# Weight-block sums for a Winograd-form down projection: added up in DRAM by accumulating transfers, instead of on VectorE

## The chip, the cores and the metric

The kernel runs on one core of a Trainium2 chip. A core has a matrix engine (TensorE, PE in the profile, with its weight loads as PEld), a vector engine (VectorE, DVE), an activation engine (ScalarE, ACT), a general engine (GpSimd, POOL) and a queue engine (SyncE, SP). They run side by side, each through its own list of instructions in order, and wait for one another by semaphores. Sixteen DMA engines move data between DRAM and the core's memory (SBUF); SP, ACT and POOL each issue transfers on a queue of their own (q1, q10 and q0 in the profile). Time is device time in microseconds (us); a difference under about 0.2% is not told from none.

## What is computed

Two layers of a hybrid decoder over 512 positions of width 1024, in float32. Each layer adds two branches to the residual x. The first mixes positions in three ways (RWKV-7, retention, spatial gating) and merges them. The second is a gated MLP, and its last matmul in the last layer, with the final norm, is the last stage here:

```python
for l in range(DEPTH):
    h = rmsnorm(x, norm1_g[l])
    p = h @ w_in[l]
    ...
    x = x + jnp.sum(gates * proj, axis=2) @ w_out[l]
    x = x + conv_ffn(rmsnorm(x, norm2_g[l]), ffn_w_up[l], ffn_conv_w[l], ffn_conv_b[l], ffn_w_down[l])
return rmsnorm(x, final_g)
```

The down projection takes 2816 inner channels (22 blocks of 128) to 1024 outputs.

## The kernel before

Every float32 product is made of three passes in a rounded format: an operand is split into a high part (`hi`, made by ACT) and a low part (`lo`, made by DVE), and `mm3` multiplies hi by hi, hi by lo and lo by hi. Weights come as units of 128 rows by 512 columns. For each unit SP loads a raw tile `wr` of 256 KB (`load`), ACT and DVE split it (`part`), and PE uses it (`unit`). A first pass over the program writes down all units in order as a plan, and the second pass loads and splits ahead of use: `AHEAD` says how many split units may stand ahead, `NRAW` and `DEEP` how many raw ones, by the pool that the stage uses; the last stage has the pool "q", with raw tiles taken in turn from the pool of three `wr` buffers and from the general pool `u`.

The last down projection is done in a two by two block form with seven products in place of eight (Winograd's form of Strassen's method). The inner channels are taken as 11 pairs of blocks; for each pair q the weights are four blocks w0 to w3 of 128 by 512 in DRAM (`wdt`): w0 and w1 are the two column halves of the first inner block, w2 and w3 those of the second. Three of the seven products take w0, w2 and w3 as they are; four take sums of blocks, `tsum`, numbered 7, 5, 6 and 4. Each sum is a tile of 256 KB in DRAM, `ts`, 44 in all. Before the change they are made by `presum`: POOL loads the four blocks into SBUF tiles `pre` (line 253), DVE makes four sums in place (lines 242 to 245), and POOL stores them (line 248). `PRE` says at which step this happens: four pairs beside the first layer's up projection (`ffn_up`, line 1071), seven beside its down projection (`ffn_down`, line 1130). The activations' side of the form is made in `halves` in the last layer's up projection, and the products are put together in `last`.

The order of instructions on each engine is not that of the program's text. A planner goes through the program with its own estimate of durations and gives each engine the instruction whose inputs and buffers are there; the text's order only ranks what is ready. Instructions under `keep_in_program_order` and those that PE issues while `pin` is set stay in the order of the text. Each engine then runs its list in that order.

What POOL does early in layer 0 matters for the change. The first norm's reciprocal root is a power on POOL (`norm_stats`, line 267), and PE then spreads it over the rows (`norm_rows`, line 272) at a fixed place among the first projections. POOL then makes the low parts of small weights (`wus`, line 487) and of the decay and rate inputs (line 511), on which PE's groups of line 533 wait. For each of four groups of heads it masks products with affine selects (lines 579 and 580). After the fourth, `solve` copies diagonal blocks (line 771), DVE runs a recursion of 31 steps, ACT and POOL copy back (lines 769 and 771), and PE goes on with line 808.

Of the kernel before, what the change touches and what calls it, by code (L numbers as in the profile page):

```python
# [8 lines left out]
F32 = mybir.dt.float32  # L9
# [10 lines left out]
NFF = 22  # L20
# [2 lines left out]
NU, NR, NFP = 31, 16, 39  # L23
FILL = (36, 2, 1)
KEPT = 6
PRE = {(0, "f", 2): 0, (0, "f", 4): 1, (0, "f", 6): 2, (0, "f", 8): 3, (0, "d", 0): 4, (0, "d", 1): 5, (0, "d", 2): 6, (0, "d", 3): 7,
       (0, "d", 4): 8, (0, "d", 5): 9, (0, "d", 6): 10}
SEQ = "0 H 0 S 0 U S U S 0 S 0 0 S 2 2 Y 0 0 2 1 2 1 2 1 2 1 2 1 2 1 1 1"
NRAW = 3
AHEAD = {None: 2, "p": 4, "r": 3, "f": 3, "u": 5, "q": 4}  # L30
DEEP = 6
EXP_HALF = math.exp(-0.5)


# [17 lines left out]
class Emit:  # L52
# [181 lines left out]
        q.dma_start(d, t)  # L234
        return d

    def presum(self, l, stage, m):

        if self.pre:
            q, b = self.pre.pop()  # L240
            V = self.nc.vector
            V.tensor_tensor(b[3], b[3], b[1], op=SUB)
            V.tensor_tensor(b[1], b[1], b[0], op=SUB)
            V.tensor_tensor(b[0], b[0], b[3], op=ADD)
            V.tensor_tensor(b[2], b[2], b[0], op=SUB)
            for p, t in zip((7, 5, 6, 4), (b[3], b[1], b[0], b[2])):
                self.tsum[q, p] = self.dp.tile([128, 512], F32, name=self.nm("ts"))
                self.nc.gpsimd.dma_start(self.tsum[q, p], t)
        q = PRE.get((l, stage, m))
        if q is not None:  # L250
            b = self.fpre.pop(0) if stage == "f" else [self.u(n="pre") for _ in range(4)]
            for i, t in enumerate(b):
                self.nc.gpsimd.dma_start(t, self.a["wdt"][0, 2 * q + i // 2][:, i % 2 * 512:i % 2 * 512 + 512])
            self.pre.append((q, b))

    def norm_new(self):
        return {"z": [], "acc": None}
# [66 lines left out]
    def run(self):  # L324
        nc, tc, a, V = self.nc, self.tc, self.a, self.nc.vector
        self.con = self.cp.tile([128, NCC], F32, name="con")
        self.pre, self.tsum = [], {}
        self.rst = self.cp.tile([128, 512], F32, name="rst")
        self.bonesR = self.cp.tile([128, 128], F32R, name="bonesR")
        self.ones = self.cp.tile([128, 128], F32R, name="ones")  # L330
        V.memset(self.rst, 1.0)
        wu = self.acc()
        for i in range(5):
            nc.tensor.matmul(wu[:, 0:256], self.rst[:, 0:128], self.rst[:, 256:512], start=True, stop=True)
        self.pc = self.sp.tile([128, 64], F32, name="g1", tag="g1", bufs=1)
        st = self.norm_new()
        xs = [self.u(n="x") for _ in range(8)]
        self.keep = True
        with tc.high_priority():
            tc.keep_in_program_order(nc.scalar.dma_start(self.pc[:, 0:8], a["pcols"][0][:, PC["n1"]:PC["n1"] + 8]))  # L340
            for j in range(8):
                tc.keep_in_program_order((nc.scalar if j in (1, 3) else nc.sync).dma_start(xs[j], a["xT"][:, j, :]))
                if self.plan and j in (0, 2, 3):
                    self.load(self.plan[self.nraw])
        tc.keep_in_program_order(nc.scalar.copy(self.small((128, 1), "ms"), self.rst[:, 0:1]))
        tc.keep_in_program_order(nc.scalar.copy(self.ones, self.rst[:, 0:128]))
        for step in "z0 w z1 z2 z3 w w z4 z5 w z6 z7 w s0 s1 s2 w s3 s4 s5 s6 s7".split():
            if step == "w":
                if self.plan:
                    if self.nraw == self.npart:  # L350
                        self.load(self.plan[self.nraw])
                    self.part(self.plan[self.npart])
            elif step[0] == "z":
                self.norm_z(st, xs[int(step[1])], "n1")
            else:
                self.norm_sq(st, xs[int(step[1])])
        self.keep = False
        self.load_pc(0)
        tc.keep_in_program_order(nc.scalar.dma_start(self.con, a["con"]))
        xd = [a["xT"][:, j, :] for j in range(8)]  # L360
        for l in range(L):
            mg = self.mixer(l, st)
            st = self.norm_new()
            x = self.wout(l, mg, xd, st)
            st["sq"] = self.split(st["acc"])
            act = self.ffn_up(l, st, x if l == L - 1 else None)
            if l == L - 1:
                self.last(act)
            else:
                st = self.norm_new()  # L370
                x, xd = self.ffn_down(l, act, x, st)
                st["sq"] = self.split(st["acc"])
            self.rp.__exit__(None, None, None)
            self.fp = None
# [683 lines left out]
    def ffn_up(self, l, st, x):  # L1058
        nc, V, A = self.nc, self.nc.vector, self.nc.scalar
        nt = [0]  # L1060
        self.xt = []

        def at(**kw):
            nt[0] += 1
            return (self.f if nt[0] <= NFP else self.r)(dt=F32R, n="ah")

        act = []
        first = self.firstF(l, (78, 79, 80), st, (3,))
        if l == 0:
            self.fpre = [[self.f(n="pre") for _ in range(4)] for _ in range(4)]  # L1070
        for i in range(NFF):
            if l == 0 and i % 2 == 0 and 2 <= i <= 10:
                self.presum(l, "f", i)
            if x and i % 2 == 1 and i < 17:
                o = self.r(n="xt")
                self.turned(o, self.r(n="xT"), x[i // 2], nc.gpsimd)
                self.xt.append(o.rearrange("p (a c d) -> p c a d", c=4, d=32))
            cs = []
            for j in (i, NFF + i):
                ps = first.pop(0) if first else self.colF(l, 78 + 2 * i + (j >= NFF))  # L1080
                u = self.u(n="fu")
                V.tensor_tensor(u, ps, self.rsF, op=MUL)  # L1082
                t = self.u(n="cv")
                A.activation(t, u, AF.Identity, scale=self.p("cw2", j), bias=self.p("cb", j))  # L1084
                V.scalar_tensor_tensor(t[:, 1:], u[:, :511], self.p("cw1", j), t[:, 1:], op0=MUL, op1=ADD)
                V.scalar_tensor_tensor(t[:, 2:], u[:, :510], self.p("cw0", j), t[:, 2:], op0=MUL, op1=ADD)
                cs.append(t)
            g, v = cs
            th = self.u(n="fth")
            A.activation(th, g, AF.Tanh, scale=0.5)  # L1090
            V.scalar_tensor_tensor(th, th, 1.0, g, op0=ADD, op1=MUL)
            V.tensor_tensor(th, th, v, op=MUL)
            if l < L - 1:
                act.append(self.split(th, at))
            elif i % 2 == 0:
                even = th
            else:
                act.append(self.halves(even, th, i // 2, at))
        return act

    def halves(self, a, b, q, at):
# [5 lines left out]
            self.s4 = self.dp.tile([128, 512], F32, name=self.nm("s4"))  # L1107
        P.dma_start(ab[:, h[0]], a[:, h[0]])
        P.dma_start(ab[:, h[1]], b[:, h[0]])
        V.tensor_tensor(s[:, h[0]], a[:, h[1]], b[:, h[1]], op=ADD)  # L1110
        V.tensor_tensor(s[:, h[1]], s[:, h[0]], a[:, h[0]], op=SUB)
        V.tensor_tensor(d[:, h[0]], b[:, h[0]], s[:, h[1]], op=SUB)
        P.dma_start(self.s4[:, h[q % 2]], d[:, h[0]])
        V.tensor_tensor(b[:, h[0]], a[:, h[0]], a[:, h[1]], op=SUB)
        return self.split(s, at), self.split(b, at), ab, self.s4

    def ffn_down(self, l, act, x, st):
# [3 lines left out]
        for m in range(8):  # L1121
            ps = self.acc()
# [4 lines left out]
            d = self.dp.tile([128, 512], F32, name=self.nm("xd"))  # L1127
            nc.gpsimd.dma_start(d, x[m])
            xd.append(d)
            self.presum(l, "d", m)  # L1130
        return x, xd


    def last(self, act):
# [27 lines left out]
            po(A.activation(t, ps, AF.Copy, scale=0.5))  # L1162
            return t

        def addx(ps, h, c):

            y = self.f(n="v")
            for j in range(4):
                v = lambda t: t[:, 128 * j:128 * j + 128].rearrange("p (a d) -> p a d", d=32)
                x = self.xt[4 * h + j][:, c]  # L1170
                V.scalar_tensor_tensor(v(y), v(ps), 0.5, x, op0=MUL, op1=ADD)  # L1171
            return y

        def plus(y, ps, z):
            return V.scalar_tensor_tensor(y, ps, 0.5, z, op0=MUL, op1=ADD)

        def square(y, s):
            return A.activation(self.u(n="sq")[:, 0:y.shape[1]], y, AF.Square, accum_out=s)  # L1178
# [32 lines left out]
        for q in range(Q):  # L1211
# [5 lines left out]
            if q % 2 or q == Q - 1:  # L1217
                s4.append(spill(act[q][3], 512 if q % 2 else 256))
            if q < 2:
                v[2, q], v[3, q] = addx(pss[5][q], 1, 2 + q), addx(pss[5][q], 1, q)  # L1220
            elif q < 4:
                v[1, q - 2] = addx(pss[4][q - 2], 0, q)
            elif q < 6:
# [5 lines left out]
        for q in range(Q):  # L1229
# [3 lines left out]
            if q < 2:  # L1233
                plus(f0[q], out[1][q], f0[q])
                plus(v[0, q], out[1][q], v[0, q])
                plus(v[3, q], out[1][q], v[3, q])
            elif q in (2, 5):
                r = q // 5
                c, ya, yb = 2 + r, v[1, r], v[2, r]
                V.tensor_tensor(ya, ya, f0[r], op=ADD)  # L1240
                V.tensor_tensor(yb, yb, f0[r], op=ADD)
                s1, b = self.small((128, 1), "fs1"), bias[:, c:c + 1]
                square(ya, ss[:, c:c + 1])
                square(yb, s1)
# [20 lines left out]
        for r in range(2):  # L1265
            for q, w in enumerate(ws, Q - KEPT):
                go(3, q, r, w)
            y, ya, b = v[3, r], v[0, r], bias[:, r:r + 1]
            po(plus(y, out[3][r], y))
            if r == 0:  # L1270
                s = self.small((128, 1), "fs1")
                po(square(y, s))
# [131 lines left out]
```

## Time and profile before

| | us |
|---|---|
| median of 3 runs (lowest, highest) | 1713.97 (1713.09, 1715.02) |
| profiled execution | 1706.19 |
| its span, first to last instruction | 1704.5 |
| PE busy | 1687.8 |
| DVE busy | 1233.0 |
| ACT busy | 798.0 |
| POOL busy | 249.8 |

The profile is one execution. A row of a group of instructions gives line, engine, operation, tiles written and read, count, busy time and mean, and then the idle time of the engine just before them with what ended it. A row of the timeline gives start and length in us first. Rows of the DMA queues give packets, MB and the share of 16 engines' time in the stretch asked for; rows of DMA issues give size and the median time from issue to landing. PE's matmuls overlap in their pipeline, so that one of 390 ns begins about 228 ns after the one before it.

### The profile page before, as it was taken

What the parts mean: (1) busy time and instruction counts of PE and PEld (TensorE: products, weight loads), DVE (VectorE), ACT (ScalarE), POOL (GpSimd) and SP (SyncE); (2) the same over time, 40 slices, a digit from 0 to 9 for tenths busy, and PEclk for the clock granted to TensorE, in tenths of its full rate; (3) what the DMA queues carried; (4) which work ended last, traced back from release to release, by engine and by line L of the source; (5) the groups of instructions that cost most, each with busy time, mean ns of one, the idle gap of its engine ahead of it and who ended that gap; (6) DMA issues with size and microseconds to landing.
All of it is one profiled execution on the core that took longest, in us unless ns stands there. A gap on an engine that the chain in (4) does not pass through costs nothing. (4 is left out here: it accounts for less than half of the span.)

```text
span 1704.5 us, 27880 instructions
## 1 busy us (share of the span) xinstructions
PE 1687.8 (99%) x10214; PEld 1379.2 (81%) x10214; DVE 1233.0 (72%) x2157; ACT 798.0 (47%) x1367; POOL 249.8 (15%) x353
## 2 busy tenths in 40 slices
PE   9999999999999999999999999999999999999998
PEld 7888777888888888888888887778888888887786
DVE  6887745578669887765568887455785698888777
ACT  6563433454255444433355634335542554444555
POOL 2121000003301200013321210000132022110110
PEclk9999999999999999999999999999999999999999
DMA  5236552524544533147742365526254444343774
GB/s 180 88 107 196 179 178 98 183 90 161 191 143 148 193 123 97 59 153 260 254 144 90 103 206 167 179 94 192 86 171 146 154 138 134 124 136 112 252 248 142
DMA packets 146649, 260.01 MB, mean 153 GB/s; under 512 B 19600, under 2 KB 39824, under 8 KB 146512
## 3 DMA queue, kind: packets, MB, share of 16 engines
q1 hardware_dynamic: 120512, 188.54, 34.9%
q0 software_dynamic: 17216, 54.28, 9.5%
q10 hardware_dynamic: 8784, 15.42, 2.5%
q8 instruction: 80, 1.31, 0.3%
q14 instruction: 57, 0.47, 0.1%
HBM read 212.94 MB, written 45.22 MB: 151 GB/s over the span
## 5 line engine op out<-in xcount | busy, mean ns | idle before, releaser
L156 PE MATMUL acc<-lo,sh 128*128 128x512 f32 x1108 | 431.8, 390 | 0.5 <-ACT sh L139 0.5
L156 PE MATMUL acc<-hi,sh 128*128 128x512 f32 x1108 | 431.9, 390 | 0.0
L156 PE MATMUL acc<-hi,sl 128*128 128x512 f32 x1108 | 430.3, 390 | 0.2 <-DVE sl L140 0.2
L139 ACT CAST sh<-wr 128x512 fp32r<-128x512 f32 (+1 forms) x375 | 228.0, 615 | 394.9 <-PE acc L156 225.2
L140 DVE TENSOR_TENSOR sl<-wr,sh 128x512 fp32r<-128x512 f32 (+1 forms) x375 | 254.8, 685 | 129.4 <-ACT sh L139 92.8
L140 DVE TENSOR_TENSOR wl<-wr,wh 128x512 fp32r<-128x512 f32 x238 | 166.4, 704 | 131.7 <-ACT wh L139 128.9
L139 ACT CAST wh<-wr 128x512 fp32r<-128x512 f32 x238 | 145.9, 618 | 228.6 <-PE acc L156 153.9
L156 PEld LDWEIGHTS acc<-lo,sh 128*128 128x128 f32 x1108 | 208.0, 188 | 44.9 <-ACT sh L139 1.2
L156 PEld LDWEIGHTS acc<-hi,sl 128*128 128x128 f32 x1108 | 208.0, 188 | 44.2 <-DVE sl L140 0.7
L156 PEld LDWEIGHTS acc<-hi,sh 128*128 128x128 f32 x1108 | 208.0, 188 | 43.3 <-issue 0.3
L156 PE MATMUL acc<-lo,wh 128*128 128x512 f32 x588 | 232.0, 395 | 0.9 <-DVE lo L215 0.8
L156 PE MATMUL acc<-hi,wl 128*128 128x512 f32 x588 | 230.4, 392 | 1.0 <-DVE wl L140 1.0
L156 PE MATMUL acc<-hi,wh 128*128 128x512 f32 x588 | 229.3, 390 | 0.0
L156 PEld LDWEIGHTS acc<-hi,wl 128*128 128x128 f32 x588 | 110.4, 188 | 27.4 <-DVE wl L140 3.8
L156 PEld LDWEIGHTS acc<-lo,wh 128*128 128x128 f32 x588 | 110.4, 188 | 25.9 <-DVE lo L215 2.0
L156 PEld LDWEIGHTS acc<-hi,wh 128*128 128x128 f32 x588 | 110.4, 188 | 22.5 <-issue 0.2
L156 PE MATMUL acc<-ah,sh 128*128 128x512 f32 x352 | 108.4, 389 | 0.0
L1084 ACT ACTIVATE cv<-fu,pc 128x512 f32<-128x512 f32 x88 | 71.6, 815 | 60.1 <-DVE fu L1082 58.8
L1082 DVE TENSOR_TENSOR fu<-acc,rsF 128x512 f32<-128x512 f32 x88 | 60.6, 689 | 39.2 <-PE acc L156 39.1
L156 PE MATMUL acc<-wl,hi 128*128 128x512 f32 x212 | 86.1, 406 | 0.0
L156 PE MATMUL acc<-wh,lo 128*128 128x512 f32 x212 | 82.8, 390 | 0.0
L156 PE MATMUL acc<-wh,hi 128*128 128x512 f32 x212 | 82.7, 390 | 0.0
(360 smaller groups left out, 2436.8 us busy)
## 6 DMA issues: line engine op xcount, KB each, us to landing
wr<-wall SPq DMA_DIRECT2D x488, 256.0 KB, 2.8
gd<-gth ACTq DMA_DIRECT2D x48, 256.0 KB, 3.1
gth<-gd POOLq DMA_DIRECT2D x48, 256.0 KB, 3.6
pre<-wdt POOLq DMA_DIRECT2D x44, 256.0 KB, 6.0
ts<-pre POOLq DMA_DIRECT2D x44, 256.0 KB, 2.6
wr<-ts SPq DMA_DIRECT2D x44, 256.0 KB, 3.8
wr<-wdn SPq DMA_DIRECT2D x40, 256.0 KB, 3.7
wr<-wdt SPq DMA_DIRECT2D x33, 256.0 KB, 3.4
```

The source lines that it names most:

```text
L139: self.kept(self.nc.scalar.copy(hi[:, :n], raw[:, :n]))
L140: self.kept(self.nc.vector.tensor_tensor(lo[:, :n], raw[:, :n], hi[:, :n], op=SUB))
L156: i = self.nc.tensor.matmul(*x, **y, **kw)
L1082: V.tensor_tensor(u, ps, self.rsF, op=MUL)
L1084: A.activation(t, u, AF.Identity, scale=self.p("cw2", j), bias=self.p("cb", j))
```

## The change

`presum` issues transfers alone. For each pair, four copies from DRAM to DRAM set up the four sums with one block each (w1, w0, w0 and w2). Then accumulating transfers, which add what they read to what lies at their target, bring in the rest: w3 into sum 7 and w1 into sum 5; then sum 7 into sum 6; then sum 6 into sum 4. That makes 44 copies and 44 accumulating transfers, all on POOL's queue, written in the text at steps 2 to 15 of the first layer's up projection, the four kinds of one pair a step apart. Their rows are split so that no piece is longer than 512 bytes (`max_dma_last_dim`). `PRE`, the tiles `pre` and DVE's sums are gone.

Such a transfer can only add, so the form's signs change: sums 7 and 5 become w1 + w3 and w0 + w1, sum 6 is w0 + w1 + w3, and sum 4 is w0 + w1 + w2 + w3. `halves` makes the activations' side with other signs (four DVE operations again, two of them with a factor of -1, and a copy on ACT where the fourth difference was), and `last` puts the products of sums 7 and 5 together with -0.5 and one subtraction.

Apart from that, `AHEAD["q"]` goes from 4 to 6 and `DEEP` from 6 to 10.

```diff
-PRE = {(0, "f", 2): 0, (0, "f", 4): 1, (0, "f", 6): 2, (0, "f", 8): 3, (0, "d", 0): 4, (0, "d", 1): 5, (0, "d", 2): 6, (0, "d", 3): 7,
-       (0, "d", 4): 8, (0, "d", 5): 9, (0, "d", 6): 10}
...
-AHEAD = {None: 2, "p": 4, "r": 3, "f": 3, "u": 5, "q": 4}
-DEEP = 6
+AHEAD = {None: 2, "p": 4, "r": 3, "f": 3, "u": 5, "q": 6}
+DEEP = 10
...
-    def presum(self, l, stage, m):
-
-        if self.pre:
-            q, b = self.pre.pop()
-            V = self.nc.vector
-            V.tensor_tensor(b[3], b[3], b[1], op=SUB)
-            V.tensor_tensor(b[1], b[1], b[0], op=SUB)
-            V.tensor_tensor(b[0], b[0], b[3], op=ADD)
-            V.tensor_tensor(b[2], b[2], b[0], op=SUB)
-            for p, t in zip((7, 5, 6, 4), (b[3], b[1], b[0], b[2])):
-                self.tsum[q, p] = self.dp.tile([128, 512], F32, name=self.nm("ts"))
-                self.nc.gpsimd.dma_start(self.tsum[q, p], t)
-        q = PRE.get((l, stage, m))
-        if q is not None:
-            b = self.fpre.pop(0) if stage == "f" else [self.u(n="pre") for _ in range(4)]
-            for i, t in enumerate(b):
-                self.nc.gpsimd.dma_start(t, self.a["wdt"][0, 2 * q + i // 2][:, i % 2 * 512:i % 2 * 512 + 512])
-            self.pre.append((q, b))
+    def presum(self, i):
+
+        g, w, Q = self.nc.gpsimd, lambda q, n: self.a["wdt"][0, 2 * q + n // 2][:, n % 2 * 512:n % 2 * 512 + 512], NFF // 2
+        add = lambda o, x: g.dma_start(o, x, accum_op=ADD, max_dma_last_dim=512)
+        if i < Q:
+            t = {p: self.dp.tile([128, 512], F32, name=self.nm("ts")) for p in (7, 6, 4, 5)}
+            for p, n in ((7, 1), (5, 0), (6, 0), (4, 2)):
+                g.dma_start(t[p], w(i, n))
+                self.tsum[i, p] = t[p]
+        if 0 <= i - 1 < Q:
+            add(self.tsum[i - 1, 7], w(i - 1, 3))
+            add(self.tsum[i - 1, 5], w(i - 1, 1))
+        if 0 <= i - 2 < Q:
+            add(self.tsum[i - 2, 6], self.tsum[i - 2, 7])
+        if 0 <= i - 3 < Q:
+            add(self.tsum[i - 3, 4], self.tsum[i - 3, 6])
...
-        if l == 0:
-            self.fpre = [[self.f(n="pre") for _ in range(4)] for _ in range(4)]
         for i in range(NFF):
-            if l == 0 and i % 2 == 0 and 2 <= i <= 10:
-                self.presum(l, "f", i)
+            if l == 0 and 2 <= i < NFF // 2 + 5:
+                self.presum(i - 2)
...
-        V.tensor_tensor(s[:, h[0]], a[:, h[1]], b[:, h[1]], op=ADD)
-        V.tensor_tensor(s[:, h[1]], s[:, h[0]], a[:, h[0]], op=SUB)
-        V.tensor_tensor(d[:, h[0]], b[:, h[0]], s[:, h[1]], op=SUB)
+        V.tensor_tensor(s[:, h[0]], b[:, h[1]], a[:, h[1]], op=SUB)
+        V.tensor_tensor(d[:, h[1]], a[:, h[0]], a[:, h[1]], op=SUB)
+        V.scalar_tensor_tensor(s[:, h[1]], d[:, h[1]], -1.0, b[:, h[1]], op0=MUL, op1=SUB)
+        V.scalar_tensor_tensor(d[:, h[0]], s[:, h[1]], -1.0, b[:, h[0]], op0=MUL, op1=SUB)
         P.dma_start(self.s4[:, h[q % 2]], d[:, h[0]])
-        V.tensor_tensor(b[:, h[0]], a[:, h[0]], a[:, h[1]], op=SUB)
+        self.nc.scalar.copy(b[:, h[0]], d[:, h[1]])
...
-            self.presum(l, "d", m)
...
-                v[2, q], v[3, q] = addx(pss[5][q], 1, 2 + q), addx(pss[5][q], 1, q)
+                v[2, q], v[3, q] = addx(pss[5][q], 1, 2 + q, -0.5), addx(pss[5][q], 1, q, -0.5)
...
-                plus(v[3, q], out[1][q], v[3, q])
+                plus(v[3, q], out[1][q], v[3, q], -0.5)
...
-                V.tensor_tensor(yb, yb, f0[r], op=ADD)
+                V.tensor_tensor(yb, yb, f0[r], op=SUB)
...
-            po(plus(y, out[3][r], y))
+            po(plus(y, out[3][r], y, -0.5))
```

More of the change, by code (lines that the diff above doesn't have):

```diff
@@ L326, in run @@
         self.con = self.cp.tile([128, NCC], F32, name="con")
-        self.pre, self.tsum = [], {}
+        self.tsum = {}
         self.rst = self.cp.tile([128, 512], F32, name="rst")
@@ L1163, in half, with addx @@
             return t
-        def addx(ps, h, c):
+        def addx(ps, h, c, scale=0.5):
             y = self.f(n="v")
@@ L1170, in addx, with plus @@
                 x = self.xt[4 * h + j][:, c]
-                V.scalar_tensor_tensor(v(y), v(ps), 0.5, x, op0=MUL, op1=ADD)
+                V.scalar_tensor_tensor(v(y), v(ps), scale, x, op0=MUL, op1=ADD)
             return y
-        def plus(y, ps, z):
-            return V.scalar_tensor_tensor(y, ps, 0.5, z, op0=MUL, op1=ADD)
+        def plus(y, ps, z, scale=0.5):
+            return V.scalar_tensor_tensor(y, ps, scale, z, op0=MUL, op1=ADD)
         def square(y, s):
```

## The prediction

> **What bounds the kernel now.** I read the page first, then stretches of the span, then what TensorE (PE) waited for, then POOL's queue and the DMA queues, because the change lives on those two.
>
> ```profile
> span 1704.5 us, 27880 instructions
> PE 1687.8 (99%) x10214; PEld 1379.2 (81%) x10214; DVE 1233.0 (72%) x2157; ACT 798.0 (47%) x1367; POOL 249.8 (15%) x353
> ```
>
> PE is the bound, with 16.7 us idle in the whole span. So nothing that shortens VectorE (DVE) or POOL work can be worth more than a few us, and a stall put into PE's queue is not won back later: it adds to the time. Stretches (length, then busy us of PE, PE's weight loads, DVE, ACT, POOL, then granted clock, DMA share, GB/s):
>
> ```profile
> core 0: us, PE busy (x) PEld busy (x) DVE busy (x) ACT busy (x) POOL busy (x), PEclk, DMA share, GB/s
> 0.00:28.00 28.00, 25.55 (x102) 19.66 (x103) 16.86 (x31) 17.65 (x31) 1.32 (x6) 1.00 0.68 222
> 0.00:72.00 72.00, 69.05 (x349) 55.30 (x350) 50.92 (x85) 45.26 (x78) 9.68 (x12) 1.00 0.47 150
> 500.00:700.00 200.00, 200.00 (x884) 165.59 (x884) 168.27 (x263) 99.16 (x154) 15.03 (x28) 1.00 0.41 136
> 700.00:900.00 200.00, 200.00 (x884) 165.63 (x883) 123.12 (x193) 78.11 (x130) 43.30 (x74) 1.00 0.55 180
> 1300.00:1500.00 200.00, 200.00 (x883) 165.43 (x882) 160.71 (x259) 92.95 (x147) 31.95 (x57) 1.00 0.42 137
> ```
>
> In 500 to 900 us, where the weight sums are made now (first up projection and first down projection), PE never idles; nor in 1300 to 1500, the second up projection. The last stage, by PE's waits from 1500 us to the end (us in total, times, longest):
>
> ```profile
> PE acc L156 <- DVE wl L140: 2.4, 2, 1.8
> PE acc L156 <- DVE sl L140: 0.8, 3, 0.3
> PE acc L156 <- ACT sh L139: 0.5, 1, 0.5
> PE sm L156 <- DVE wl L140: 0.2, 1, 0.2
> ```
>
> That is 3.9 us, all that more units ahead could remove.
>
> **Where the change really stands.** The accumulating transfers read and write DRAM alone, so no buffer holds them back, and POOL is idle early. In the compiled order of the changed kernel they are not beside the first up projection: all 88 stand at the head of POOL's queue, before and between the first steps of layer 0's mixer. Some of its rows, with the semaphores that each waits for:
>
> ```
> 6 L242 DMACopy ts_1149_5611<-wdt 128x512
> 47 L238 DMACopy ts_1252_6031<-wdt 128x4x128 [waits DMASW1_49]
> 48 L263 ISA
> 49 L263 TensorTensor rs_80_327<-ms_79_325,con_78 128x4 [waits DMAHW2_49,DVE_49]
> 85 L242 DMACopy ts_1399_6664<-wdt 128x512 [waits DMASW0_49]
> 86 L507 TensorTensor lo_96_390<-wax_94_386,hi_95_389 128x512 [waits Activation_49]
> 101 L238 DMACopy ts_1401_6666<-ts_1400_6665 512x128 [waits DMASW5_49]
> 102 L575 TensorScalarAffineSelect Y_144_560<-Y_144_560 64x1024 [waits Activation_49]
> ```
>
> From the ninth on, each transfer waits for the one eight before it (semaphores DMASW0 to 7 in turn), so POOL runs at the pace at which transfers land, and what stands behind it waits too. Row 49 is the first norm's power (L267 of before), behind 42 transfers; row 86 is the second low part of the decay and rate inputs (L511 of before), behind 73. When before does the same work (POOL's rows, then PE's):
>
> ```profile
> 26.80 1.04 POOL L267 TENSOR_TENSOR rs<-ms,con 128x4 f32<-128x4 f32 x1 [26.29 <-DVE ms L265]
> 40.63 1.28 POOL L511 TENSOR_TENSOR lo<-wax,hi 128x512 fp32r<-128x512 f32 x1 [0.73 <-ACT hi L510]
> 131.15 2.59 POOL L771 COPY cs<-GB 32x1024 f32<-32x1024 f32 x2
> 191.62 2.39 POOL L771 COPY GB<-cs 32x1024 f32<-32x1024 f32 x2 [55.87 <-DVE cs L797]
> ```
>
> ```profile
> 28.03 0.60 PE L272 MATMUL sm<-con,rs 128*128 128x128 f32 x4
> 28.39 0.48 PE L156 MATMUL acc<-lo,wh 128*128 128x512 f32 x1
> 47.31 0.39 PE L156 MATMUL acc<-hi,wl 128*128 128x512 f32 x1
> 47.54 0.39 PE L533 MATMUL sm<-lo,wus 128*128 128x512 f32 x1
> 200.26 0.42 PE L808 MATMUL sm<-cs,GB 32*32 32x32 f32 x28
> ```
>
> PE takes the norm's rows 0.2 us after the power ends, in a fixed place. The 84 matmuls from 28.39 to 47.31 give 0.228 us each. In the changed order the second group that needs row 86 is PE's row 284, 112 + 2 + 82 matmuls behind the norm's rows: unstalled, PE would be there at 28.4 + 196 x 0.228 = 73.1 us. (The order has already moved these groups back, from rows 172 and 174 to 200 and 284; that room is in the 73.1. The norm's rows were not moved.)
>
> **The price of a transfer.** The nearest rows are the busiest stretch of POOL's queue (755 to 870 us):
>
> ```profile
> DMA packets 11811, 28.24 MB, mean 246 GB/s; under 512 B 1773, under 2 KB 2541, under 8 KB 11804
> q0 software_dynamic: 5120, 16.78, 42.0%
> q1 hardware_dynamic: 6396, 10.85, 29.9%
> q10 hardware_dynamic: 288, 0.52, 1.4%
> ```
>
> and a stretch with many 512-byte rows (200 to 300 us):
>
> ```profile
> DMA packets 10880, 14.49 MB, mean 145 GB/s; under 512 B 1467, under 2 KB 5051, under 8 KB 10865
> q1 hardware_dynamic: 9412, 11.16, 36.2%
> q10 hardware_dynamic: 1133, 2.06, 5.5%
> q0 software_dynamic: 320, 1.05, 3.5%
> q8 instruction: 12, 0.20, 0.8%
> bkS<-tr SPq DMA_DIRECT2D x32, 32.0 KB, 2.4
> yF<-tr SPq DMA_DIRECT2D x12, 64.0 KB, 2.0
> ```
>
> First: 73.3% of 115 us is 84.3 us for 28.24 MB, 335 GB/s with all 16 engines at work; a 256 KB copy is 0.78 us of them. Second: 5051 - 1467 = 3584 packets of 512 B carry 1.84 MB; the other 12.65 MB cost 37.8 us at 335 GB/s; of the 46.0 us busy 8.2 remain, times 16 engines over 3584: 37 ns each. An accumulate of 256 KB goes out in 512-byte rows (128x4x128 and 512x128 above): 512 packets over 16 engines, 1.17 us if one pass is all. No row of before shows an accumulate. Its lower bound is the plain copy's 0.78 us; its upper is three passes one after the other (read source, read target, write target), 3.5 us. I take two passes, 2.34 us, since a copy's 37 ns already holds one read beside one write and the second read is what comes on top.
>
> The Trainium skill, page "Collectives: The Full Stack", section "The bandwidth ceiling: the fold count and why AG ≠ RS ≠ AR", says a reducing transfer runs at half the rate of a copy because it reads two sources. No run here shows it; put on the plain copy it would make 1.56 us, and the sum below about 1753 us, an estimate.
>
> **Sum.** The DMA engines are full from the start: POOL has eight transfers in flight, and x, weights and constants fill 0.68 x 28 = 19.0 us of the first 28 already. Until PE's row 284, x and weights want 0.47 x 72 = 33.8 us of engines. By row 85's wait 65 transfers have landed, 38 copies and 27 accumulates (counted in the order). With a us for an accumulate: start 1.5 us (estimate) + 33.8 + 38 x 0.78 + 27a + L511 and its hand-over 2 = 66.9 + 27a, against 73.1. Delay: 27a - 6.2. At 2.34 that is 57 us; at 0.78, 15; at 3.5, 88. The same count at the norm (27 copies, 7 accumulates): 1.5 + 19.0 + 21.1 + 16.4 = 58 us instead of 26.8, so some 31 of the 57 are lost there.
>
> Then the solve. The order puts 69 matmuls of filler (15.7 us) ahead of the last chunk's products that stood behind them, while the solve's matmuls (L808) stay at PE's row 924. In before its inputs are ready at 191.62 + 2.39 = 194.0 and PE arrives at 200.26: 6.3 us of room. 15.7 - 6.3 = 9.4 us of stall; DVE has six weight splits fewer beside its recursion, so I take 5, between 0 and 9. POOL's own backlog ends earlier than that: after row 85 come 3 copies and 12 accumulates, 30 us, while three chunks of products remain.
>
> Edits with one answer: the 44 subtractions and additions and the 88 old transfers leave 500 to 900 us: nothing, PE is full there, and so are the buffers they free. The re-signed halves: four DVE operations as before, one of them now a copy on ACT more; hidden, as PE is full at 1300 to 1500 with ACT at 93 of 200 us; without cover, some 11 x 0.5 us. The re-signed scales and the subtraction in the last stage: same count, nothing. Ahead 6 and deep 10: between -3.9 us and, if early splits push others back, as much lost; I take -2, as three buffers each still cap half of the units.
>
> 57 + 5 - 2 = +60 us. The profiled execution took 1706.19 us around its span of 1704.5; the median of the runs is 7.8 us above it, 1713.97; to that I add: **1774 us**.
>
> On the power itself:
>
> ```profile
> L267 POOLq MODIFY_POOL_CONFIG  x2: 11/11/11, 0.8 to 0.8; - x2
> ```
>
> In before this set-up has 26 us until its use; changed, it stands right ahead of row 49. The Trainium skill, "GPSIMD Engine Reference", section 2.1 "Instruction dispatch", gives about 6 us for the first call of a freshly loaded routine. This trace can't show that, the load being hidden; by it the sum would be 1780.
>
> **Rivals.**
> 1. Accumulates as cheap as copies or one pass (0.78 to 1.17 us): 15 to 25 + 3, so 1732 to 1742; middle 1736. For it: the engines need not be the limit of the added read. Against: 512-byte rows are already dearer than copies.
> 2. Accumulates dearer than three passes, say 5 us (latency of read, add and write in DRAM): 27 x 5 - 6.2 + 3 = +132, 1846. No row excludes it.
> 3. Other side: the train is hidden. POOL reaches row 49 in time only if 34 transfers land in the 26.8 - 1.5 - 19.0 = 6.3 us of engine time left, 0.185 us each. Below that price nothing is lost, the last stage gains 3.9, 1710. Against: every 256 KB in this trace costs four times as much.
>
> **How the numbers follow.** Forecast (1.17 to 3.5 us per accumulate) 0.62; rival 1 0.18; rival 2 0.13; rival 3 0.05, and 0.02 for ends that meet within 0.2%, about what a measurement of this kernel can tell. Range: low end the copy's price with no solve stall and 3.9 gained, 15 - 4 = +11, 1725; high end three passes and 9 of solve stall, 88 + 9 = +97, rounded up to 1815. It leaves out rivals 2 and 3. Faster 0.05, same 0.02, slower 0.93.
>
> **What would show it.** POOL's first 100 us: DMA issues from about 1 us, the power near 58 us instead of 26.8, PE idle ahead of the norm's transposes for some 30 us and ahead of the groups on wus for 25 more; DMA share near 1 until about 130 us; L808 released by the copies of the solve. Wrong if PE's idle before 200 us stays below 10 us, if POOL's transfers wait elsewhere, or if the accumulates land at another pace than 2.3 us of engine time each.

## The result, and the profile after

The changed kernel takes 1761.47 us (median; 1754.49 to 1765.82) where the kernel before, run beside it, takes 1713.02: a ratio of 1.0284, 95% interval 1.0256 to 1.0312, so 48 us are lost. The profiled execution took 1765.82 us, 59.6 more than the one of before. The change is slower by about as much as was forecast (+60, 1774 us), but only part of the way there was the one forecast: the late norm and the stall at the solve came, the 25 us at the groups on `wus` did not, and late loads and a lower clock filled their room.

The span, the busy times and the granted clock by slices, from the page of the kernel after:

```profile
span 1764.1 us, 27709 instructions
PE 1705.1 (97%) x10214; PEld 1389.6 (79%) x10214; DVE 1212.0 (69%) x2113; ACT 802.8 (46%) x1378; POOL 277.0 (16%) x353
PEclk8899999999999999999999999999999999999999
```

PE has the same 10214 matmuls. It idles 59.0 us instead of 16.7 (+42.3) and is busy 17.3 us longer; together that is the 59.6. The second part comes from the clock. Stretches of the kernel after (length, busy us of PE, PE's weight loads, DVE, ACT, POOL, then granted clock, DMA share, GB/s):

```profile
0.00:28.00 28.00, 19.00 (x53) 13.59 (x54) 10.04 (x15) 11.62 (x19) 14.05 (x28) 0.82 0.98 308
28.00:72.00 44.00, 27.32 (x105) 22.11 (x104) 19.46 (x32) 15.35 (x27) 32.08 (x36) 0.76 1.16 254
72.00:130.00 58.00, 49.54 (x258) 39.48 (x258) 31.14 (x49) 22.77 (x38) 35.11 (x36) 0.95 1.30 247
130.00:200.00 70.00, 69.27 (x460) 56.37 (x460) 57.25 (x95) 41.97 (x72) 24.00 (x22) 0.97 0.49 132
200.00:260.00 60.00, 53.68 (x347) 42.93 (x346) 48.34 (x104) 20.01 (x33) 2.32 (x2) 0.94 0.55 178
700.00:900.00 200.00, 200.00 (x884) 165.68 (x883) 113.17 (x179) 76.61 (x125) 3.58 (x7) 1.00 0.34 102
```

Most is lost before PE reaches the solve's matmuls, which it does at 252.39 us (line 804) where before it did at 200.26 (line 808): 52.1 of the 59.6 us. Up to 72 us PE runs 53 + 105 matmuls where before it ran 349. Each stretch's busy time times what its clock lacks gives 3.4 + 6.6 + 2.5 + 2.1 + 3.2 = 17.8 us, the 17.3 of busy time. From 700 to 900 DVE does 10 us less and POOL 40 less, and PE is as full as before. What PE waited for in the whole span (us, times, longest):

```profile
PE sm L268 <- POOL rs L263: 11.5, 1, 11.5
PE acc L154 <- ACT wh L137: 6.6, 2, 5.7
PE sm L804 <- DVE cs L790: 5.4, 1, 5.4
PE sm L259 <- DMA con<-con: 5.2, 1, 5.2
PE acc L154 <- ACT sh L137: 4.9, 3, 4.0
PE sm L584 <- ACT Y L572: 4.2, 2, 3.5
```

POOL's power (line 263) is the longest single wait, but only about a quarter of the new idle time. ACT's `wh` and `sh` are the high parts of weights, and ACT itself waited for the raw tile. In the timeline of ACT, and then PE, of the kernel after (start, length, and in brackets the idle time before with its releaser):

```profile
24.23 0.62 ACT L137 CAST wh<-wr 128x512 fp32r<-128x512 f32 x1 [5.23 <-DMA wr<-wall]
88.51 0.62 ACT L137 CAST wh<-wr 128x512 fp32r<-128x512 f32 x1 [6.27 <-DMA wr<-wall]
```

```profile
24.90 0.79 PE L154 MATMUL acc<-lo,wh 128*128 128x512 f32 x1 [5.68 <-ACT wh L137]
40.06 1.84 PE L259 MATMUL sm<-con,sq 128*128 128x1 f32 x8 [5.16 <-DMA con<-con]
57.91 1.11 PE L268 MATMUL sm<-con,rs 128*128 128x128 f32 x4 [11.52 <-POOL rs L263]
92.34 0.50 PE L154 MATMUL acc<-lo,sh 128*128 128x512 f32 x1 [4.03 <-ACT sh L137]
111.83 0.39 PE L529 MATMUL sm<-lo,wus 128*128 128x512 f32 x1
252.39 1.93 PE L804 MATMUL sm<-cs,GB 32*32 32x32 f32 x128 [5.43 <-DVE cs L790]
```

The last stage gained nothing either. From 1550 us to the end PE's waits add up to 6.1 us, where before they were 3.9; the two longest:

```profile
PE sm L154 <- DVE wl L138: 2.6, 3, 2.2
PE sm L154 <- ACT v L1156: 2.3, 1, 2.3
```

POOL's queue, in its timeline:

```profile
1.32 4.30 POOL L242 DMA_DIRECT2D ts<-wdt  x8 [0.81 <-POOLq L1386]
56.27 1.58 POOL L263 TENSOR_TENSOR rs<-ms,con 128x4 f32<-128x4 f32 x1
100.67 1.29 POOL L507 TENSOR_TENSOR lo<-wax,hi 128x512 fp32r<-128x512 f32 x1
134.57 1.01 POOL L238 DMA_DIRECT2D ts<-ts  x1 [2.07 <-DMA ts<-ts]
```

The transfers stand where the order put them, from 1.3 us on, and last until 134.6 us. The loads beside them land late. Issues in 0 to 56 us (KB each, median us from issue to landing), first before, then after:

```profile
wr<-wall SPq DMA_DIRECT2D x23, 256.0 KB, 2.9
x<-xT SPq DMA_DIRECT2D x6, 256.0 KB, 6.1
con<-con ACTq DMA_DIRECT2D x1, 469.5 KB, 4.8
```

```profile
wr<-wall SPq DMA_DIRECT2D x13, 256.0 KB, 8.7
x<-xT SPq DMA_DIRECT2D x6, 256.0 KB, 12.9
con<-con ACTq DMA_DIRECT2D x1, 469.5 KB, 12.4
```

So two theories stand beside each other. Theory Q: the loss is POOL's queue, in which the norm's power stands behind the transfers. Theory B: the loss is the transfers' load on DRAM and the DMA engines, by which loads with no slack come late. The forecast had been built on Q and on the price of an accumulate. The expectations also name S, the new signs and the deeper look-ahead of the last stage.

### The profile page after: what moved, and what is told of

It is laid out like the page before. It is cut to its first block, busy times and chain, and to the rows that moved or that the text cites. A ratio compares the mean times of both kernels' runs of the same rounds, so it can differ in the third digit from the quotient of the medians.

```text
span 1764.1 us, 27709 instructions
## 1 busy us (share of the span) xinstructions
PE 1705.1 (97%) x10214; PEld 1389.6 (79%) x10214; DVE 1212.0 (69%) x2113; ACT 802.8 (46%) x1378; POOL 277.0 (16%) x353
## 4 chain that ended last, share of the span: by engine, by line
PE 75%; DMA 10%; DVE 8%; issue 2%; ACT 2%; SPq 1%; POOL 1%; ACTq 0%; POOLq 0%; DVEq 0%
PE acc L154 68%; DMA wr<-wall 4%; DMA ts<-wdt 3%; DVE wl L138 2%; PE sm L660 2%; PE sm L154 2%; DMA wr<-wdt 1%; PE sm L913 1%; DVE sl L138 1%; DVE TMP L784 1%; ACT wh L137 1%; DVE cs L786 1%; DMA tr<-bkT 1%; SPq L228 1%; PE sm L567 1%
## 5 line engine op out<-in xcount | busy, mean ns | idle before, releaser
L154 PE MATMUL acc<-lo,wh 128*128 128x512 f32 x588 | 236.5, 402 | 8.4 <-ACT wh L137 6.6
L154 PE MATMUL acc<-hi,wh 128*128 128x512 f32 x588 | 233.0, 396 | 0.0
```

The lines of the kernel that those rows point to most:

```text
L154: i = self.nc.tensor.matmul(*x, **y, **kw)
```

## The experiments

The kernel before was run on the same chip beside each of them (1706 to 1709 us), and each ratio is against those runs.

**The look-ahead alone** (the kernel before, with two numbers changed):

```diff
-AHEAD = {None: 2, "p": 4, "r": 3, "f": 3, "u": 5, "q": 4}
-DEEP = 6
+AHEAD = {None: 2, "p": 4, "r": 3, "f": 3, "u": 5, "q": 6}
+DEEP = 10
```

> The kernel before with ahead 6 and deep 10 in the last stage and nothing else. Q: 1711 us, between 1709 and 1717, since PE waits only 3.9 us in that stage. S: more than 4 us away from before on either side.

Measured: 1707.75 us, ratio 0.9996 (0.9982 to 1.0009). This part is worth nothing that can be told; the interval leaves room for 3 us of gain and 1.5 of loss.

**The transfers placed where the text has them** (the change, with every one of the 88 transfers kept in program order on POOL):

```diff
-        add = lambda o, x: g.dma_start(o, x, accum_op=ADD, max_dma_last_dim=512)
+        kept = self.tc.keep_in_program_order
+        add = lambda o, x: kept(g.dma_start(o, x, accum_op=ADD, max_dma_last_dim=512))
...
-                g.dma_start(t[p], w(i, n))
+                kept(g.dma_start(t[p], w(i, n)))
```

> The changed kernel with its 88 transfers kept behind what the text issues before them on POOL, so that they run beside the first up projection; all else as in the change. Theory Q (the loss is POOL's early steps standing behind the transfers): no loss, 1711 us, between 1707 and 1717. Rival B (the transfers slow the weight loads wherever they run; in a step of the up projection of 9.1 us they want some 3 us for copies and 8 for accumulates beside 3.7 of weights): PE stalls there, 1730 us or more. Rival S (signs, ahead 6 and deep 10 cost something of their own): over 1717 with no PE stall in the up projection, the stall in the last stage.

Measured: 1732.64 us, ratio 1.0139 (1.0115 to 1.0163). Half of the loss is gone, and the rest has moved. Since no operand holds them, the transfers now ran from 457 us, beside the matmul of `w_out` that comes ahead of the up projection. PE's waits and two stretches of this kernel:

```profile
PE acc L154 <- DVE xi L1048: 15.1, 6, 3.8
```

```profile
456.00:550.00 94.00, 78.88 (x311) 61.79 (x310) 47.64 (x72) 33.57 (x53) 58.66 (x73) 0.91 1.20 277
550.00:600.00 50.00, 50.00 (x222) 41.42 (x221) 43.27 (x69) 25.10 (x41) 16.80 (x18) 1.00 1.05 222
```

Neither PE's waits nor DVE's in that stretch name POOL, so the waits point to B and not to Q, which had been given 1711 us. B's time (1730 or more) came true, but not at its place: it had PE stall in the up projection. `xi` is the residual input that DVE adds to each product of `w_out`. It is loaded one tile at a time just ahead of use, and landed 7.3 us after issue instead of 3.6. That the late `xi` makes the whole loss can't be read from the waits alone: DVE's own list there has 6.0 us for the loads of `xi` and 31.3 us for ACT's `sh`. From 550 us on, at a DMA share of 1.05, PE loses nothing. Two experiments separate the place from the load.

**The same, with xi loaded early** (the placed version; all eight loads issued ahead of the loop):

```diff
+        xis = [self.u(n="xi") for _ in range(8)] if l == 0 else []
+        for m, xi in enumerate(xis):
+            nc.sync.dma_start(xi, xd[m])
         for m in range(8):
-            xi = self.u(n="xi")
-            nc.sync.dma_start(xi, xd[m])
+            xi = xis[m] if xis else self.u(n="xi")
+            if not xis:
+                nc.sync.dma_start(xi, xd[m])
```

> The placed version, with all eight loads of the first layer's residual input xi issued ahead of w_out's loop instead of one by one in it; the transfers still run beside w_out from 457 us. If the placed version's loss of 24 us is the late xi (15.1 us of PE's waits on DVE's xi sums, and some 9 us of lower clock that follows them), this one stands at 1709 to 1715 us on a chip where the kernel before has 1709, and the waits on xi are gone from PE's list at the same DMA share. If weights are late as well, or if the clock falls with the DMA share alone, it stays at 1720 us or more.

Measured: 1705.73 us, ratio 0.9990 (0.9977 to 1.0003). The same stretch of this kernel:

```profile
456.00:550.00 94.00, 93.53 (x412) 77.14 (x413) 65.56 (x100) 42.56 (x69) 58.95 (x73) 1.00 1.19 276
```

The waits on `xi` are gone from PE's list, and with them the whole 24 us: one kind of load without slack had made the loss. The DMA share is as high as in the placed version, the weights land as late (6.4 us against 6.5), PE is full, and the clock is 1.00.

**The transfers inside the up projection** (the placed version; each group waits for its step's activation):

```diff
             if l == 0 and 2 <= i < NFF // 2 + 5:
+                self.tc.keep_in_program_order(nc.gpsimd.tensor_copy(self.small((128, 1), "gate"), act[-1][0][:, 0:1]))
                 self.presum(i - 2)
```

> The placed version, with one small copy on POOL ahead of each group of transfers that reads the first column of the up projection's latest activation, so that the group cannot start before its own step of the up projection: the 88 transfers run inside the up projection instead of beside w_out. Theory Q (POOL's queue) and theory B with slack (a transfer costs time only where the loads beside it are needed at once) both give the time of the kernel before, about 1709 us on a chip where that is 1709, since in the placed version PE was busy for 50.00 of the 50 us from 550 to 600 at a DMA share of 1.05. If the weights of the up projection are late beside the train, 1720 us or more, with idle time of PE ahead of the up projection's matmuls released by DMA, and if the slower clock follows the DMA share itself rather than PE's idle time, a granted clock under 0.95 there without idle time.

Measured: 1708.42 us, ratio 1.0002 (0.9991 to 1.0013). The transfers ran from 533 to 671 us, and here too PE is full:

```profile
550.00:600.00 50.00, 50.00 (x222) 41.39 (x221) 38.84 (x60) 23.10 (x36) 31.34 (x40) 1.00 1.22 278
```

So the signs, the look-ahead, the DRAM sums themselves and the DVE work they save add up to nothing that can be told (within about 2 us); the whole loss of the change is the place in which its transfers run.

**The transfers behind the norm's power** (the change; no transfer is issued ahead of the power):

```diff
-        nc.gpsimd.tensor_tensor(self.rsT, ms, self.c("mhalf")[:, 0:4], op=POW)
+        self.power = nc.gpsimd.tensor_tensor(self.rsT, ms, self.c("mhalf")[:, 0:4], op=POW)
...
-                self.presum(i - 2)
+                with self.tc.issue_after(self.power.ins):
+                    self.presum(i - 2)
```

> The changed kernel with the 88 transfers queued behind the first norm's power on POOL and still ahead of the steps that follow. Q: the stall at the norm's rows (about 30 us in the changed kernel) is gone; the train ends some 30 us later, and POOL's masks for the solve and the solve come late instead, 8 to 25 us; 1728, between 1718 and 1740. B: the same bytes run against the same loads, at least 1750.

Measured: 1736.42 us, ratio 1.0170 (1.0143 to 1.0196), 29 us. The power was out on time, at 25.99 us, and the transfers followed until 155 us. ACT's timeline and PE's:

```profile
56.11 0.62 ACT L137 CAST wh<-wr 128x512 fp32r<-128x512 f32 x1 [5.50 <-DMA wr<-wall]
63.64 0.62 ACT L137 CAST wh<-wr 128x512 fp32r<-128x512 f32 x1 [4.83 <-DMA wr<-wall]
```

```profile
65.92 0.79 PE L154 MATMUL acc<-lo,sh 128*128 128x512 f32 x1 [9.98 <-ACT sh L137]
225.11 1.93 PE L804 MATMUL sm<-cs,GB 32*32 32x32 f32 x128 [5.51 <-DVE cs L790]
```

The time is inside what Q was given (1718 to 1740) and below what B was given (1750 or more), so by time alone this was a point for Q. PE's waits say otherwise. None of them is for POOL; late weights stop PE for 10 us in one piece. That is B's mechanism at a smaller price than expected, and Q alone cannot be the cause. The solve's stall of 5.5 us, which Q had put down to POOL's late masks, is there too; it tells for neither, since the forecast derives it from the order of PE's rows.

**POOL's queue alone** (the kernel before, without any new transfer; POOL subtracts a tile from itself 42 times, and the power needs the zero that results):

```diff
+            hold = self.small((128, 512), "rsF", bufs=1)
+            self.tc.keep_in_program_order(nc.gpsimd.memset(hold, 0.0))
+            for _ in range(42):
+                self.tc.keep_in_program_order(nc.gpsimd.tensor_tensor(hold, hold, hold, op=SUB))
+            self.tc.keep_in_program_order(nc.gpsimd.tensor_tensor(hold[:, 0:4], hold[:, 0:4], self.c("mhalf")[:, 0:4], op=ADD))
+            self.mh = hold[:, 0:4]
...
-        nc.gpsimd.tensor_tensor(self.rsT, ms, self.c("mhalf")[:, 0:4], op=POW)
+        nc.gpsimd.tensor_tensor(self.rsT, ms, self.mh, op=POW)
```

> The kernel before, without any of the 88 transfers, in which POOL is held ahead of the first norm's power by 42 subtractions of a 128x512 tile from itself (1.28 us each by L507's rows, 54 us) whose result, zero, is added to the power's exponent, so that the power starts near 56 us as in the change and all loads find the memory free. Theory Q (POOL's queue alone makes the loss): PE waits from its own 28 us until 57 us at the norm, 27 to 29 us in one piece, some 5 to 9 us more go to the lower clock after it, and the time is 1738 to 1750 us where the kernel before has 1709. With the version whose transfers stand behind the power (27 us slower by the loads alone) this tells how the change's 48 us are made: if the two losses add up to more than 48, they overlap, since loads that are late anyway hide a late power. If the work behind the norm has slack to win the delay back, less than 1730 us; then the loads and not the queue make most of the change's loss. If the clock falls only beside a high DMA share, the granted clock stays at 1.00 after PE's wait.

Measured: 1746.99 us, ratio 1.0227 (1.0202 to 1.0253), 39 us. PE's timeline, and the stretch around the wait:

```profile
37.06 1.87 PE L264 MATMUL sm<-con,sq 128*128 128x1 f32 x8 [6.36 <-DVE sq L223]
58.30 1.12 PE L283 MATMUL sm<-con,rs 128*128 128x128 f32 x4 [14.08 <-POOL rs L278]
```

```profile
37.00:58.00 21.00, 7.15 (x20) 5.51 (x20) 4.42 (x6) 0.62 (x1) 19.59 (x19) 0.58 0.13 46
```

The late power alone puts PE's norm rows at 58.30, where the change has them at 57.91, and costs 39 of the 48 us that the change costs. One thing went otherwise than meant: DVE's operations beside POOL's ran at half speed (the weights' low parts 1424 ns instead of 687), so PE came to the norm later by itself and its wait is 14 us and not 28. The end of the wait is the power's all the same. So Q alone costs about 39 us (with whatever DVE's slower operations add behind the norm, which no run separates), and B alone about 29, the solve's stall included. Together they are not 68 us but the change's 48. That a late load hides a late power, and the reverse, is how I read this; in the change's own profile PE's rows ahead of the norm are late by loads, and the wait for POOL is the shorter for it.

**Copies in place of accumulates** (the change, with the same 88 transfers, none of which adds):

```diff
-        add = lambda o, x: g.dma_start(o, x, accum_op=ADD, max_dma_last_dim=512)
+        add = lambda o, x: g.dma_start(o, x)
```

> The change with each accumulating transfer turned into a plain copy of the same block to the same place, so that the number, order and bytes of the transfers stay and only the adding is gone; the sums hold the last term alone and the output is not the reference's. If the accumulate's own price (2.15 us of packet time against 0.78 us of a copy) sets the loss, the train is over near 80 to 95 us in place of 135 us, the power is out near 40 us in place of 56 us, and the time is 1735 to 1745 us. If only the number and places of the transfers count, it stays at 1761 us.

Measured: 1747.70 us, ratio 1.0234 (1.0219 to 1.0250), between the two times given. The power was out at 48.24 us and not near 40. PE's wait for it is short all the same:

```profile
PE sm L268 <- POOL rs L263: 2.1, 1, 2.1
```

So 40 us are lost here with 2.1 us of waiting for POOL: late loads had already held PE back nearly as long as the queue held the power.

**The 44 copies alone** (the change without its accumulating transfers):

```diff
-        add = lambda o, x: g.dma_start(o, x, accum_op=ADD, max_dma_last_dim=512)
+        add = lambda o, x: None
```

> The change without its 44 accumulating transfers: the 44 copies alone are issued, so the blocks that the last stage reads hold one term and not the sum, and the output is not the reference's. Theory Q: the power of the first norm still stands behind the same number of rows less the accumulates, so it starts when some 35 copies are through, near its old place of 28 us to 35 us, and the time falls to about 1720 to 1735 us. Theory B: the train is over near 60 us in place of 135 us, the loads of x, constants and first weights are still late by some 5 us each, and the time is 1725 to 1740 us. Above 1750 us the accumulates are not what costs.

Measured: 1735.73 us, ratio 1.0161 (1.0143 to 1.0178). That is inside B's range and at the end of Q's, so it does not tell them apart. The power was out at 47.44 us, not at 28 to 35, and PE waited 5.7 us for it. The DMA queue of POOL over the whole span, in the kernel after, with 88 copies and with 44:

```profile
q0 software_dynamic: 36928, 54.28, 12.6%
```

```profile
q0 software_dynamic: 16160, 54.28, 9.1%
```

```profile
q0 software_dynamic: 13696, 42.74, 7.1%
```

Of the 48 us, 27 are there with 44 plain copies, 40 with 88, and the adding costs only about 9 (each ratio less one, times the time of before). The 88 copies differ from the change in one thing more than the adding: they go out without the split into 512-byte rows, in fewer packets. The run with longer rows, below, shows that the split alone is worth nothing that can be told. The last of the new transfers was issued at 134.6, 102.2 and 49.8 us. Cutting the train from 134 us to 50 thus saved 21 us of 48; the 50 us that were left still cost 27. The stall of 5.4 us at line 804 is in the version with 88 copies too (PE at 238.75), and not in the one with 44, whose order of PE is another.

**Longer rows** (the change with 2048 for 512 in `max_dma_last_dim`):

> The changed kernel with rows of 2048 bytes in place of 512 in the accumulating transfers; same order on all engines. Q with two passes per accumulate: 256 KB cost 1.56 us of the engines instead of some 2.2, 27 of them stand ahead of PE's row 284, so about 16 us come back, 1745. If an accumulate in such rows costs no more than a copy, 0.78 us, 1724. If its price goes by elements and not by packets, no change, 1761. B (bytes alone count): no change, 1761.

Measured: 1761.70 us, ratio 1.0315 (1.0289 to 1.0341). Its q0 and PE's first waits:

```profile
q0 software_dynamic: 20032, 54.28, 10.9%
```

```profile
PE sm L268 <- POOL rs L263: 10.5, 1, 10.5
PE acc L154 <- ACT sh L137: 6.6, 3, 5.3
PE acc L154 <- ACT wh L137: 6.0, 3, 5.3
```

The time is the one given for B or for a price by elements. The packets did get cheaper, though, about as Q had put it, so a price by elements is out. Cheaper packets gain nothing: the last transfer is issued at 125.2 instead of 134.6 us, and PE waits for weights somewhat longer instead.

## Where the prediction was right, and where not

1. *Where the transfers run.* Right: at the head of POOL's queue, from 1.32 us, eight in flight, the last at 134.6 us ("until about 130"). PE idles 34.9 us before 200 us, far over the 10 named as a sign of being wrong.
2. *The price of a transfer.* In the kernel before, q0 takes 9.5% of 1704.5, 161.9 us, of which the 88 removed transfers are 69 at 0.78. With 93 for what stays, the change's 222.3 leave 129 for the new ones; 44 copies at 0.78 taken off, an accumulate is 2.15 us of packet time, shared by 16 engines, against the 2.34 assumed (an estimate, since 0.78 is itself an average). The same sum for 88 copies gives 0.75 each (0.78 assumed), and with 2-KB rows it gives 1.46 for an accumulate. The Trainium skill, "Collectives: The Full Stack", section "The bandwidth ceiling: the fold count and why AG ≠ RS ≠ AR", has a reduce at half a copy's rate, which by the copy's price here would be 1.56 us, an estimate; the 1.46 with 2-KB rows agrees, the 2.15 with 512-byte rows does not.
3. *The sum of engine times.* This step failed: it took the engines as full and let their times add, and so had line 507 done at 66.9 + 27 x 2.34 = 130 us. It ran at 100.67. The queues of the kernel after in 0 to 130 us (packets, MB, share of 16 engines' time) show why:

```profile
q0 software_dynamic: 25134, 22.27, 91.4%
q1 hardware_dynamic: 5577, 10.16, 23.4%
q10 hardware_dynamic: 1008, 1.66, 3.7%
```

They add up to 118.5%, so the times of packets overlap, and the train went on at 133.3 / 88 = 1.51 us per transfer. Up to 101 us the three shares add up to 115%, 116 us of packet time, where the forecast's sum had 33.8 + 29.6 + 63.2 = 127: of the 28 us by which line 507 came earlier, some 15 are overlap and some 10 less packet time. With the prices nearly right, the pace was not: 130 us for what took 102.
4. *The norm.* The power was forecast at 58 us and ran at 56.27, and PE's rows behind it came 29.9 us late (57.91 against 28.03) where 31 were forecast. But PE did not idle for 30 us there. It idled 11.5; the rest had been lost before, at late weights and constants and at a clock of 0.82 and less. The version with POOL held shows that the queue alone would have done it.
5. *The groups on wus, 25 us more.* Wrong. No wait shows there: line 507 was done at 101.96 and PE came to row 284 at 111.83 by itself. That is 38.7 us late instead of 57, and the 8.8 beyond the norm are late weights (4.03 at 92.34) and the clock.
6. *The solve.* Forecast 5, measured 5.43, at the place named. That it is so close is luck, as 5 was picked between 0 and 9. The releaser was DVE's transpose behind the recursion (line 790, which is line 794 of before) and not the copies of ACT and POOL.
7. *What the sum left out.* From row 284 to line 804 another 8.0 us (52.1 - 38.7 - 5.4), most of it PE's waits for ACT's `Y` (4.2 us where before had 0.5) and a clock of 0.97 (3.9 us by the rule above); and behind it 7.5, of which the clock of 0.90 in the 25 us after the stall is 2.5 and the last stage's waits 2.2; the rest was not located. The forecast had no term for late loads and none for the clock. They filled the room of the 25 us that never came, so the profiled loss agrees with the sum (59.6 against 60) by errors that cancel; by the medians it is 48.
8. *Edits at nothing, and the last stage.* Right for the first (1.0002 with the transfers inside the up projection); the 2 us of gain from deeper look-ahead can't be told from none (0.9982 to 1.0009).
9. *The rivals.* A cheap accumulate was to give 1732 to 1742 us. With copies in their place, which the forecast took as the lower bound, the loss is still 40 us, where rival 1's own sum has 18 at 0.78. The price decides much less than the forecast and both its neighbours assumed. The hidden train (rival 3) does exist, but by place and not by price.
10. *A first call.* The Trainium skill, "GPSIMD Engine Reference", section 2.1 "Instruction dispatch", has about 6 us for a freshly loaded routine. The trace does not agree here: with its set-up of 0.5 us right ahead of it, the power took 1.58 us at 56.27, against 1.04 before.

Three things stay open: how the 48 us divide between queue and loads while both act; how much of them is the order of PE's rows, which no run changes alone (the 5.4 to 5.5 us at line 804 stand in the change and in three versions of it, with longer rows, with 88 copies and behind the power, and in no other run); and what the unlocated 3 us of point 7 are.

## What to carry to other kernels

A transfer between two DRAM tensors has no buffer to wait for in the core's memory, so a scheduler that issues what is ready puts it at the head of its queue; give it an operand, or an order, that ties it to the stage where it is to run. Before moving transfers beside a stage, look for that stage's loads with the least time between issue and use (here x, constants and first weights at the start, `xi` beside `w_out`): the same train cost 48 us, 24 us or nothing, and issuing eight loads earlier made the difference between 24 and nothing. Work taken from an engine that is not the bound gained nothing here.

## What was not expected of the hardware

- In these runs the granted clock follows PE's own idleness and not the DMA load: 0.58 in 37 to 58 us of the version with POOL held, at a DMA share of 0.13 and PE busy a third of the time; 1.00 at a share of 1.19 with xi early. A stall so costs more than its length: 31.2 us of idle time came with 9.5 us of longer busy time in the version with POOL held. (PE's busy time is modelled: it also differs by 6.0 us in the version gated into the up projection, which lost nothing; but the clock's rows, worked out as above, give 9.3 here.) The Trainium skill, "TensorE: Matmul & The Clock Gate", section "Part 1: The HAM clock gate (the "warmup" mystery)", says that the array drops to half its clock after an idle window of about 3.4 us and is released by as long a busy one; the 0.58, beside waits of 6.4 and 14.1 us, agrees.
- An accumulating transfer in 512-byte rows mostly occupies POOL's issue for 1.0 to 1.4 us (0.81 to 0.84 in 2-KB rows), where a copy mostly takes 0.52 to 0.58.
- POOL's subtractions of 128x512 tiles doubled the time of DVE's operations beside them: 1424 ns against 687 for the same subtraction on DVE.
